# A short first chunk, and the recurrent stage's elementwise work moved from GpSimd to VectorE and ScalarE

## The chip, the core and the metric

The kernel runs on one core of a Trainium2 chip. The metric is device time in microseconds (us), from one launch. Engines are named as the profile names them: PE is TensorE, PEld its weight loads, DVE is VectorE, ACT is ScalarE, POOL is GpSimd, and SP is SyncE, which here issues all DMAs.

## What is computed

One layer of a hybrid decoder for a prompt of 4096 positions and for 8 single-token samples. All is fp32. The reference, cut to what matters here:

```python
xn = rms_norm(x, norm_pre)                       # x: 4096 x 1024 (prompt), 8 x 1024 (samples)
proj = xn @ w_in                                 # 1024 x 2304
x_rnn, g_rnn, q, k, v, g_att = split(proj)       # 512, 512, 512, 128, 128, 512
xc = causal_conv(x_rnn, width 4)                 # depthwise, along positions
r, i = sigmoid(blockdiag(xc) + b_a), sigmoid(blockdiag(xc) + b_x)
a = exp(-8 r softplus(-lam))
h_t = a_t h_{t-1} + sqrt(1 - a_t^2) (i_t xc_t)   # scan over positions
rnn_out = h * silu(g_rnn)
att_out = window_attention(q, k, v, window 128, sinks, bias) * silu(g_att)
y = x + rms_norm(concat(rnn_out, att_out) @ w_out, norm_post)
```

The samples go through the same layer, each from its own convolution state, recurrent state and key/value window. The new states and windows are outputs too.

## The kernel before, in words

Positions lie along the columns, and a *chunk* is the unit of all stages. `chunk_list` (L38) cuts 4096 positions into ten chunks of 384 (`STEP`) and a last one of 256; the eight samples ride as columns 256 to 263 of that last chunk. A chunk is thus 384 or 264 columns wide. Every fp32 product is made of three matmuls of rounded high and low parts (`mm3`, L121 to L124).

**Stage A, the recurrent heads**, one chunk after another. `load_A` (L146) loads x in tiles of 128 rows (the samples are a tile of 8 rows), takes the mean square (ACT, L161; in the first chunk's second tile DVE, L157), its root on POOL (L141), and scales the tile by it: on DVE in the first chunk (L164), on POOL in all others (L166). `prep_A` transposes the tile on PE (L176) and splits it into high (ACT, L179) and low parts (DVE, L180), which are also stored to DRAM (`xT_d`, L182) for stage B. `proj_A` makes two projections for each of four groups c of 128 channels (L122 to L124; 8 x 24 matmuls a chunk), evacuates them (ACT, L298, L302, L316), makes three convolution taps on DVE (L304; for the samples L309), and splits the result xc into xk (L312, L313). `rnn_A` makes the two gate products from xk (24 matmuls a chunk), the tanh and exp on ACT (L333 to L338), and on DVE and POOL the pieces of the recurrence: L339, L341 and L342 on DVE, `aa` (L340) on POOL. `scan_A` takes the square root on ACT (L348), then for each c multiplies `ix` by it (POOL, L350), scans (DVE, L352), and multiplies by the gate (POOL, L361); SP stores the result to `mix_d` (L362). The tiles named thi in the trace are `ix`. The projections of the very first group are L210 to L213, in another order.

The eight weight blocks of stage A (512 KB each) are loaded, rounded (ACT, L111, or DVE, L109) and their low parts taken (DVE, or POOL, L112) during the first chunk.

**Stage B, attention**, again chunk by chunk: ten projections of 24 matmuls (V, K, four Q, four G), and a unit for each pair of key head and 128-query block: scores (L601, L602), masked minimum and softmax on DVE and ACT (L619 to L632), transposes (L635), triangular cuts on POOL (L654, L656), the product with the values (L661), and the gate (POOL, L676). kt (L484, L486, L524) holds split keys, sq (L564 to L567) split queries. The ten weight blocks of stage B are loaded from the end of stage A on; their low parts are taken on POOL (L112). The samples' keys, values, queries and gates are taken out of the projections' last 8 columns (L531, L546, L571, L584).

**Stage C, the output product**: eight blocks of w_out are loaded, `mix_d` is read back and split (`prep_B`, L189, L193, L195), and each tile of 128 positions is multiplied (L817 to L819), normalized, added to x and stored. `attend_sample` runs the samples' attention in five pieces between chunks and stores it to `mix_d`; the samples' tile is put between the two prompt tiles of the chunk that carries them, and that chunk's last tile ends the kernel.

What sets the order: `A_ORDER` (L33), `B_FIRST` (L35) and `B_ORDER` (L36) are the orders in which a chunk's pieces are emitted, P a projection, L the x loads and X a quarter of the preparation of the next chunk, R the gates and S the scans; U units, M their gates.

```python
A_ORDER = "P1 L P0 P2 R1 X0 R0 P3 X1 R2 X2 R3 S X3".split()
```

The build then orders each engine's queue by a timeline of its own (`schedule_with_timeline_sim=True`), so that pieces that follow each other here are interleaved in the trace. Each queue runs in its order. PSUM has four projection buffers in stage A and two in stage B.

Of the kernel before, what the change touches and what calls it, by code (L numbers as in the profile page):

```python
# [12 lines left out]
AF = mybir.ActivationFunctionType  # L13
ALU = mybir.AluOpType
# [10 lines left out]
NSAMP = 8  # L25
SEQ = 4096
STEP = 384
# [8 lines left out]


def chunk_list():  # L38
    out = [(t, min(STEP, SEQ - t), 0) for t in range(0, SEQ, STEP)]
    out[-1] = out[-1][:2] + (NSAMP,)  # L40
    return out


@with_exitstack
def hymba_kernel(ctx: ExitStack, tc: tile.TileContext, ins, outs):
    nc = tc.nc
# [9 lines left out]
    w_out_v = w_out[0].rearrange("(e p) d -> p e d", p=P)  # L56

    chunks = chunk_list()
    NCH = len(chunks)

    act = nc.scalar.activation
# [16 lines left out]
    def ps_s(n):  # L78
        if phase[0] == "A":
            return ps[1].tile([P, 1024], F32, tag="s", name=n, bufs=1)  # L80
        return ps[0].tile([P, 1024], F32, tag="s", name=n, bufs=2)
# [15 lines left out]
    mix_d = [dram.tile([P, KD, n + s], F32, name=f"mix_d{i}") for i, (_, n, s) in enumerate(chunks)]  # L97
# [23 lines left out]
    def mm3(out, wh, wl, xh, xl, first, last):  # L121
        nc.tensor.matmul(out, wh, xh, start=first, stop=False)  # L122
        nc.tensor.matmul(out, wh, xl, start=False, stop=False)  # L123
        nc.tensor.matmul(out, wl, xh, start=False, stop=last)  # L124
# [10 lines left out]
    def rstd(pool, ss, rows, n):  # L135
        nc.vector.tensor_scalar(ss[:rows], ss[:rows], EPS, None, op0=ALU.add)
        return root(pool, ss, rows, n)

    def root(pool, ss, rows, n):
        rs = pool.tile([P, 1], F32, tag="rs", name=f"rs_{n}", bufs=4)  # L140
        nc.gpsimd.tensor_tensor(rs[:rows], ss[:rows], mhalf[:rows], op=ALU.pow)  # L141
        return rs


    def load_A(pool, ci):
        t0, npt, ns = chunks[ci]  # L146
        tiles = [(x_p[t0 + i * P:t0 + (i + 1) * P, :], P, i * P) for i in range(npt // P)]
        if ns:
            tiles.append((x_s, ns, npt))
        xn = []  # L150
        for j, (src, rows, off) in enumerate(tiles):
            xs = pool.tile([P, D], F32, tag="xs", name=f"xs_{ci}_{j}", bufs=4)
            nc.sync.dma_start(xs[:rows], src)
            ss = pool.tile([P, 1], F32, tag="ss", name=f"ss_{ci}_{j}", bufs=4)
            if ci == 0 and j == 1:
                sq = pal.tile([P, D], F32, tag="uu", name=f"sq_{ci}_{j}", bufs=1)
                nc.vector.tensor_tensor_reduce(sq[:rows], xs[:rows], xs[:rows], op0=ALU.mult, op1=ALU.add,  # L157
                                               scale=1.0 / D, scalar=0.0, accum_out=ss[:rows])
            else:
                sq = pool.tile([P, D], mybir.dt.bfloat16, tag="sq", name=f"sq_{ci}_{j}", bufs=1)  # L160
                act(sq[:rows], xs[:rows], AF.Square, scale=1.0 / 32.0, accum_out=ss[:rows])  # L161
            rs = rstd(pool, ss, rows, f"{ci}_{j}")
            if ci == 0:
                nc.vector.tensor_scalar(xs[:rows], xs[:rows], rs[:rows], None, op0=ALU.mult)  # L164
            else:
                nc.gpsimd.tensor_scalar(xs[:rows], xs[:rows], rs[:rows], 1.0, op0=ALU.mult, op1=ALU.mult)  # L166
            xn.append((xs, rows, off))
        return xn

# [28 lines left out]
    cms = [tc.tile_pool(name=n, bufs=1) for n in ("pa_late", "pa", "prep")]  # L198
    pal, pa, prep = [c.__enter__() for c in cms]
    xn = load_A(prep, 0)  # L200

    def project2(w1, w2, xs, W, n, wait=False):
# [73 lines left out]
    at = spp.pop()  # L276
# [44 lines left out]
    def rnn_A(pool, ci, c, uu, xc, xk, sg):  # L321
        t0, npt, ns = chunks[ci]
        W = npt + ns
        pg = ps_s(f"gt_{ci}_{c}")
        for g in range(2):
            o = pg[:, g * 512:g * 512 + W]
            mm3(o, gwh[:, 2 * c + g, :], gwl[:, 2 * c + g, :], xk[:, 0, :W], xk[:, 1, :W], True, True)

        def wt(tag, bufs=2, pool=pool):
            return pool.tile([P, STEP], F32, tag=tag, name=f"{tag}_{ci}_{c}", bufs=bufs)[:, :W]  # L330

        thr, thi = wt("thr", 3, pal), wt("thi", 4, pal)
        act(thr, pg[:, 0:W], AF.Tanh, scale=0.5, bias=hba[:, c:c + 1])  # L333
        act(thi, pg[:, 512:512 + W], AF.Tanh, scale=0.5, bias=hbx[:, c:c + 1])

        tt, aa = wt("tt", 2, pal), wt("aa", 4, pal)
        act(tt, thr, AF.Tanh, scale=sp2[:, c:c + 1], bias=sp2[:, c:c + 1])
        act(thr, thr, AF.Exp, scale=sp4n[:, c:c + 1], bias=sp4n[:, c:c + 1])  # L338
        nc.vector.scalar_tensor_tensor(thr, thr, 1.0, tt, op0=ALU.add, op1=ALU.mult)  # L339
        nc.gpsimd.tensor_scalar(aa, thr, -1.0, 1.0, op0=ALU.mult, op1=ALU.add)  # L340
        nc.vector.scalar_tensor_tensor(uu[:, c, :W], thr, 2.0, thr, op0=ALU.subtract, op1=ALU.mult)  # L341
        nc.vector.scalar_tensor_tensor(thi, thi, 1.0, xc[:, :W], op0=ALU.add, op1=ALU.mult)  # L342
        return aa, thi, sg

    def scan_A(pool, ci, uu, parts):
        t0, npt, ns = chunks[ci]
        W = npt + ns
        act(uu[:, :, :W], uu[:, :, :W], AF.Sqrt, scale=-0.25)  # L348
        for c, (aa, ix, sg) in enumerate(parts):
            nc.gpsimd.tensor_mul(ix, ix, uu[:, c, :W])  # L350
            hh = pal.tile([P, STEP], F32, tag="hh", name=f"hh_{ci}_{c}", bufs=4)
            nc.vector.tensor_tensor_scan(hh[:, :npt], aa[:, :npt], ix[:, :npt], hprev[c] if ci else 0.0,  # L352
                                         op0=ALU.mult, op1=ALU.add)
            hprev[c] = const.tile([P, 1], F32, tag=f"hl{c}", name=f"hl_{ci}_{c}", bufs=2)
            nc.gpsimd.tensor_copy(hprev[c], hh[:, npt - 1:npt])
            if ns:
                o = hh[:, npt:W]
                nc.vector.tensor_mul(o, aa[:, npt:W], h0T[:, c, :])
                nc.vector.tensor_add(o, o, ix[:, npt:W])
                nc.gpsimd.tensor_copy(hs[:, c, :], o)  # L360
            nc.gpsimd.tensor_mul(hh[:, :W], hh[:, :W], sg[:, :W])  # L361
            nc.sync.dma_start(mix_d[ci][:, c, :], hh[:, :W])  # L362


# [76 lines left out]
    for ci in range(NCH):  # L441
        for item in A_ORDER:
            f, s = item[0], st[ci]
            c = int(item[1:] or 0)
# [237 lines left out]
    def attend_sample(pool):  # L682
# [51 lines left out]
        at = pool.tile([P, 4, NSAMP], F32, name="at_s")  # L734
# [2 lines left out]
                act(at[par * HD:(par + 1) * HD, 2 * kv:2 * kv + 2, :],  # L737
                    pov[kv * HD:(kv + 1) * HD, par, 2 * kv:2 * kv + 2, :], AF.Copy)
        nc.vector.scalar_tensor_tensor(at, at, 0.5, sgS, op0=ALU.mult, op1=ALU.mult)
        n = chunks[-1][1]  # L740
        nc.sync.dma_start(mix_d[-1][:, 4:8, n:n + NSAMP], at)

    for c in reversed(pcms):
        c.__exit__(None, None, None)
# [26 lines left out]

    wC = [load_w_out(e) for e in range(8)]
    sample = attend_sample(pb)
    turn = 0
    for ci in range(NCH):
        t0, npt, ns = chunks[ci]
        mh, ml = prep_B(ci, mix_d[ci], True, range(4))
        tiles = [(x_p[t0 + i * P:t0 + (i + 1) * P, :], y_p[t0 + i * P:t0 + (i + 1) * P, :], P, i * P)
                 for i in range(npt // P)]
# [9 lines left out]
            tiles.insert(1, (x_s, y_s, NSAMP, 0))  # L789
        for j, (xsrc, ydst, rows, off) in enumerate(tiles):  # L790
            n = f"{ci}_{j}"
            final = ci == NCH - 1 and j == len(tiles) - 1
            xr = stage.tile([P, D], F32, tag="ws", name=f"xr2_{n}")[:rows]
            nc.sync.dma_start(xr, xsrc)
            if final:
# [47 lines left out]
            rs = root(const, ss[:, 0:1], rows, f"c{n}")  # L843
# [4 lines left out]
                    nc.sync.dma_start(ydst[:, c[0]:c[1]], o)  # L848
            if not final:
                nc.sync.dma_start(ydst, xr)  # L850
        if ci:
            next(sample, None)
    for c in reversed(pcms):
        c.__exit__(None, None, None)
# [22 lines left out]
def build(nc, arrays):  # L877
    args = []
    for name in _INS + ['onehot']:
        a = arrays[f"in_{name}_dram"]  # L880
        args.append(nc.dram_tensor(f"in_{name}_dram", a.shape, mybir.dt.from_np(a.dtype), kind="ExternalInput").ap())
    res = []
    for i, (shape, dtype) in enumerate(_OUTS):
        res.append(nc.dram_tensor(f"out_{i}_dram", shape, F32, kind="ExternalOutput").ap())
    with tile.TileContext(nc, schedule_with_timeline_sim=True) as tc:
        hymba_kernel(tc, args, res)
# [13 lines left out]
```

## Time and profile before

| | us |
|---|---|
| runs, median of 3 (lowest to highest) | 1454.05 (1452.31 to 1455.19) |
| the profiled execution's own time | 1454.09 |
| its span, first to last instruction | 1452.4 |
| PE busy in the span | 1408.3 |
| DVE, ACT, POOL busy | 908.6, 798.7, 604.6 |

A share of busy time says how much an engine works, not whether it sets the end. For that one looks for stretches in which the engine that works most stands still, and for what ended its wait. The granted clock beside a stretch is the mean of TensorE's clock in it, as a share of 2.4 GHz. By PE's lines, stage A runs to some 475 us, stage B to some 1100 us, and stage C to the end.

### The profile page before, as it was taken

What the parts mean: (1) busy time and instruction counts of PE and PEld (TensorE: products, weight loads), DVE (VectorE), ACT (ScalarE), POOL (GpSimd) and SP (SyncE); (2) the same over time, 40 slices, a digit from 0 to 9 for tenths busy, and PEclk for the clock granted to TensorE, in tenths of its full rate; (3) what the DMA queues carried; (4) which work ended last, traced back from release to release, by engine and by line L of the source; (5) the groups of instructions that cost most, each with busy time, mean ns of one, the idle gap of its engine ahead of it and who ended that gap; (6) DMA issues with size and microseconds to landing.
All of it is one profiled execution on the core that took longest, in us unless ns stands there. A gap on an engine that the chain in (4) does not pass through costs nothing.

```text
span 1452.4 us, 24152 instructions
## 1 busy us (share of the span) xinstructions
PE 1408.3 (97%) x8127; PEld 1326.6 (91%) x8127; DVE 908.6 (63%) x2108; ACT 798.7 (55%) x2055; POOL 604.6 (42%) x1026
## 2 busy tenths in 40 slices
PE   6999999999988889999999999999999999999998
PEld 5999999999988889999999999999988888888886
DVE  5788777777878756576575575575665445334433
ACT  4656656666645566766776776776864222222211
POOL 3366665555656633544543543543762000000000
PEclk9999999999999999999999999999999999999999
DMA  8343354443324520221212212212336534433431
GB/s 271 127 157 133 131 168 148 142 152 120 122 73 145 184 79 31 99 85 67 99 46 76 98 42 79 98 38 70 107 111 196 172 131 145 141 135 131 146 130 60
DMA packets 115029, 170.24 MB, mean 117 GB/s; under 512 B 12214, under 2 KB 98822, under 8 KB 114906
## 3 DMA queue, kind: packets, MB, share of 16 engines
q1 hardware_dynamic: 114906, 168.71, 34.6%
q8 instruction: 64, 1.05, 0.3%
q14 instruction: 59, 0.48, 0.1%
HBM read 100.19 MB, written 68.50 MB: 116 GB/s over the span
## 4 chain that ended last, share of the span: by engine, by line
PE 83%; DVE 5%; ACT 4%; DMA 3%; issue 3%; POOL 1%; SPq 1%; POOLq 0%; DVEq 0%; ACTq 0%
PE out L817 8%; PE out L818 8%; PE out L819 8%; PE pr L122 6%; PE pr L124 6%; PE pr L123 6%; PE pga L122 4%; PE pga L123 4%; PE pga L124 4%; PE pq L122 4%; PE pq L123 4%; PE pq L124 4%; PE po L661 3%; PE S L601 2%; PE S L602 2%
## 5 line engine op out<-in xcount | busy, mean ns | idle before, releaser
L123 PE MATMUL pr<-xl,wh_in 128*128 128x384 f32 (+1 forms) x688 | 231.6, 337 | 0.0
L124 PE MATMUL pr<-xh,wl_in 128*128 128x384 f32 (+1 forms) x688 | 228.9, 334 | 0.0
L122 PE MATMUL pr<-xh,wh_in 128*128 128x384 f32 (+1 forms) x688 | 218.7, 336 | 0.9 <-ACT xc L302 0.6
L817 PE MATMUL out<-wh_out,xh_mix_d 128*128 128x512 f32 (+1 forms) x520 | 201.0, 387 | 0.0
L818 PE MATMUL out<-wl_out,xh_mix_d 128*128 128x512 f32 (+1 forms) x520 | 200.9, 386 | 0.0
L819 PE MATMUL out<-wh_out,xl_mix_d 128*128 128x512 f32 (+1 forms) x520 | 200.9, 386 | 0.0
L141 POOL TENSOR_TENSOR rs_c<-ssc,mhalf 128x1 f32<-128x1 f32 (+1 forms) x33 | 20.4, 620 | 322.5 <-DVE ssc L840 294.6
L836 ACT ACTIVATE sqc<-out 128x512 bf16<-128x512 f32 (+2 forms) x67 | 39.2, 585 | 194.6 <-PE out L819 184.4
L627 ACT ACTIVATE tt<-tt,nm 128x129 f32<-128x129 f32 x256 | 100.0, 393 | 77.2 <-DVE nm L624 76.7
L839 DVE TENSOR_TENSOR out<-out,gpost 128x512 f32<-128x512 f32 (+1 forms) x65 | 45.4, 698 | 144.2 <-ACT sqc L836 143.6
L123 PEld LDWEIGHTS pr<-xl,wh_in 128*128 128x128 f32 x688 | 131.3, 191 | 0.7 <-issue 0.7
L122 PEld LDWEIGHTS pr<-xh,wh_in 128*128 128x128 f32 x688 | 129.8, 191 | 2.1 <-ACT xc L302 1.8
L124 PEld LDWEIGHTS pr<-xh,wl_in 128*128 128x128 f32 x688 | 131.2, 191 | 0.3 <-issue 0.2
L122 PE MATMUL pq<-xh_B,wh_in 128*128 128x384 f32 (+1 forms) x352 | 119.5, 339 | 7.7 <-DVE kt L486 4.8
L123 PE MATMUL pga<-xl_B,wh_in 128*128 128x384 f32 (+1 forms) x352 | 119.1, 338 | 0.0
L123 PE MATMUL pq<-xl_B,wh_in 128*128 128x384 f32 (+1 forms) x352 | 118.9, 338 | 0.0
L124 PE MATMUL pq<-xh_B,wl_in 128*128 128x384 f32 (+1 forms) x352 | 118.6, 337 | 0.0
L304 DVE SCALAR_TENSOR_TENSOR xc<-xr,cT,xc 128x384 f32<-128x384 f32 (+1 forms) x132 | 113.0, 862 | 8.6 <-ACT xc L302 5.9
L122 PE MATMUL pga<-xh_B,wh_in 128*128 128x384 f32 (+1 forms) x352 | 118.3, 336 | 0.0
L124 PE MATMUL pga<-xh_B,wl_in 128*128 128x384 f32 (+1 forms) x352 | 117.5, 334 | 0.0
L817 PEld LDWEIGHTS out<-wh_out,xh_mix_d 128*128 128x128 f32 x520 | 97.6, 188 | 19.8 <-issue 0.2
L819 PEld LDWEIGHTS out<-wh_out,xl_mix_d 128*128 128x128 f32 x520 | 97.7, 188 | 19.6
(258 smaller groups left out, 3711.2 us busy)
## 6 DMA issues: line engine op xcount, KB each, us to landing
xs<-in_x_prompt_dram SPq DMA_DIRECT2D x32, 512.0 KB
xr<-in_x_prompt_dram SPq DMA_DIRECT2D x32, 512.0 KB
out_dram<-xr SPq DMA_DIRECT2D x31, 512.0 KB
xT_d<-xh SPq DMA_DIRECT2D x80, 192.0 KB
xT_d<-xl SPq DMA_DIRECT2D x80, 192.0 KB
xf_mix_d<-mix_d SPq DMA_DIRECT2D x80, 192.0 KB
xh_B<-xT_d SPq DMA_DIRECT2D x80, 192.0 KB
xl_B<-xT_d SPq DMA_DIRECT2D x80, 192.0 KB
```

Source lines behind the costliest of these rows:

```text
L122: nc.tensor.matmul(out, wh, xh, start=first, stop=False)
L123: nc.tensor.matmul(out, wh, xl, start=False, stop=False)
L124: nc.tensor.matmul(out, wl, xh, start=False, stop=last)
L304: nc.vector.scalar_tensor_tensor(xc[:, :npt], xr[:, t:t + npt], cw[:, t, c:c + 1], xc[:, :npt], op0=ALU.mult, op1=ALU.add)
L601: nc.tensor.matmul(o, qa, kt[:, kv, 0, kr], start=True, stop=False)
L627: act(tt[:, g, 0:P + 1], tt[:, g, 0:P + 1], AF.Exp, scale=-1.0, bias=nm[:, g:g + 1], accum_out=sm[:, g:g + 1])
L661: nc.tensor.matmul(pog[:, :, r], v.rearrange("p l d -> p (l d)"), w[:, :, r], start=i == 0, stop=i == 2)
L817: nc.tensor.matmul(p, a, wh, start=st, stop=False)
L818: nc.tensor.matmul(p, a, wl, start=False, stop=False)
L819: nc.tensor.matmul(p, b, wh, start=False, stop=sp)
L836: act(sq[:rows, :c[1] - c[0]], p[:rows], AF.Square, scale=1.0 / 32.0, accum_out=ss[:rows, i:i + 1])
L839: nc.vector.tensor_mul(po[i][:rows], p[:rows], gpost[:rows, c[0]:c[1]])
```

## The change

The short chunk, with the samples, becomes the first one; stage C takes it last. In stage A four kinds of operation change their engine: the scaling of x from POOL to ACT, and `aa`, `ix` times the root, and the scan's product with the gate from POOL to DVE. POOL keeps the root of the mean square, small copies and the weights' low parts. The chunk order of stages A and B is 0 to 10 as before, now with widths 264, 384, ..., 384.

```diff
 def chunk_list():
-    out = [(t, min(STEP, SEQ - t), 0) for t in range(0, SEQ, STEP)]
-    out[-1] = out[-1][:2] + (NSAMP,)
-    return out
+    first = SEQ % STEP
+    return [(0, first, NSAMP)] + [(t, STEP, 0) for t in range(first, SEQ, STEP)]
...
             if ci == 0:
                 nc.vector.tensor_scalar(xs[:rows], xs[:rows], rs[:rows], None, op0=ALU.mult)
             else:
-                nc.gpsimd.tensor_scalar(xs[:rows], xs[:rows], rs[:rows], 1.0, op0=ALU.mult, op1=ALU.mult)
+                act(xs[:rows], xs[:rows], AF.Copy, scale=rs[:rows])
...
-        nc.gpsimd.tensor_scalar(aa, thr, -1.0, 1.0, op0=ALU.mult, op1=ALU.add)
+        nc.vector.tensor_scalar(aa, thr, -1.0, 1.0, op0=ALU.mult, op1=ALU.add)
...
-            nc.gpsimd.tensor_mul(ix, ix, uu[:, c, :W])
+            nc.vector.tensor_mul(ix, ix, uu[:, c, :W])
...
-            nc.gpsimd.tensor_mul(hh[:, :W], hh[:, :W], sg[:, :W])
+            nc.vector.tensor_mul(hh[:, :W], hh[:, :W], sg[:, :W])
...
-        n = chunks[-1][1]
-        nc.sync.dma_start(mix_d[-1][:, 4:8, n:n + NSAMP], at)
+        n = chunks[0][1]
+        nc.sync.dma_start(mix_d[0][:, 4:8, n:n + NSAMP], at)
...
-    for ci in range(NCH):
+    order = [*range(1, NCH), 0]
+    for ci in order:
...
-            final = ci == NCH - 1 and j == len(tiles) - 1
+            final = ci == order[-1] and j == len(tiles) - 1
...
-        if ci:
+        if ci != order[0]:
             next(sample, None)
```

## Rows read from the trace of the kernel before

**Rows 1.** The page's part 1: each engine's busy time, share, instructions.

```profile
PE 1408.3 (97%) x8127; PEld 1326.6 (91%) x8127; DVE 908.6 (63%) x2108; ACT 798.7 (55%) x2055; POOL 604.6 (42%) x1026
```

**Rows 2.** Busy time by stretch: PE, PEld, DVE, ACT, POOL, granted clock, DMA, GB/s.

```profile
99.00:386.00 287.00, 285.85 (x1684) 280.44 (x1683) 228.91 (x361) 182.49 (x315) 176.49 (x213) 1.00 0.41 141
...
415.00:428.00 13.00, 9.21 (x34) 7.93 (x33) 11.06 (x21) 4.54 (x9) 4.57 (x8) 0.74 0.22 76
...
459.00:472.00 13.00, 8.51 (x43) 7.99 (x44) 13.00 (x19) 3.30 (x6) 11.12 (x14) 0.74 0.49 149
...
492.00:503.00 11.00, 6.24 (x27) 6.07 (x26) 10.86 (x18) 3.34 (x7) 8.95 (x14) 0.69 0.28 83
...
514.00:527.00 13.00, 8.43 (x40) 8.12 (x39) 9.12 (x30) 10.85 (x36) 4.80 (x3) 0.74 0.01 1
...
1038.00:1066.00 28.00, 23.56 (x174) 22.45 (x173) 16.08 (x50) 21.42 (x61) 20.09 (x26) 0.94 0.35 118
```

**Rows 3.** Waits of PE: us in total, times, the longest.

```profile
PE gt L122 <- DVE xk L312: 6.4, 2, 3.9
PE pq L122 <- DVE kt L486: 4.8, 1, 4.8
...
PE S L601 <- DVE sq L566: 3.5, 1, 3.5
PE gt L123 <- DVE xk L313: 2.4, 3, 1.3
```

**Rows 4.** Timeline of DVE from 403 us: start, duration, operation, count.

```profile
408.40 0.59 DVE L304 SCALAR_TENSOR_TENSOR xc<-xr,cT,xc 128x384 f32<-128x384 f32 x1
...
410.29 7.52 DVE L304 SCALAR_TENSOR_TENSOR xc<-xr,cT,xc 128x384 f32<-128x384 f32 x4
417.73 0.34 DVE L312 CAST xk<-xc 128x384 fp32r<-128x384 f32 x1
```

**Rows 5.** Timeline of POOL in the same stretch.

```profile
410.65 1.13 POOL L166 TENSOR_SCALAR xs<-xs,rs 128x1024 f32<-128x1024 f32 x1
411.75 1.96 POOL L361 TENSOR_TENSOR hh<-hh,sg 128x384 f32<-128x384 f32 x2
```

**Rows 6.** Groups of DVE, 36 to 475 us: busy us, mean ns, idle before.

```profile
L304 DVE SCALAR_TENSOR_TENSOR xc<-xr,cT,xc 128x384 f32<-128x384 f32 x120 | 102.8, 863 | 8.6 <-ACT xc L302 5.9 <-POOL aa L340 2.6
L352 DVE TENSOR_TENSOR_SCAN hh<-aa,hl,thi 128x384 f32<-128x384 f32 x36 | 55.5, 1563 | 2.7 <-POOL thi L350 2.7
...
L313 DVE TENSOR_TENSOR xk<-xc,xk 128x384 fp32r<-128x384 f32 x40 | 22.5, 563 | 0.3
```

**Rows 7.** Timeline of PE: three matmuls in a row, the first of 264 columns.

```profile
473.99 0.28 PE L124 MATMUL pr<-xh,wl_in 128*128 128x264 f32 x1
474.11 0.34 PE L124 MATMUL pv<-xh_B,wl_in 128*128 128x384 f32 x1
474.28 0.33 PE L122 MATMUL pv<-xh_B,wh_in 128*128 128x384 f32 x1
```

**Rows 8.** Groups of POOL, 36 to 475 us.

```profile
L350 POOL TENSOR_TENSOR thi<-thi,uu 128x384 f32<-128x384 f32 x40 | 51.8, 1326 | 23.9 <-ACT uu L348 23.9
L361 POOL TENSOR_TENSOR hh<-hh,sg 128x384 f32<-128x384 f32 x40 | 49.4, 1246 | 0.0
L166 POOL TENSOR_SCALAR xs<-xs,rs 128x1024 f32<-128x1024 f32 x28 | 39.9, 1426 | 0.2
...
L340 POOL TENSOR_SCALAR aa<-thr 128x384 f32<-128x384 f32 x40 | 27.0, 675 | 106.8 <-DVE thr L339 106.8
```

**Rows 9.** A group of ACT, 36 to 475 us.

```profile
L161 ACT ACTIVATE sq<-xs 128x1024 bf16<-128x1024 f32 x28 | 29.5, 1053 | 9.3 <-DMA xs<-in_x_prompt_dram 9.1
```

**Rows 10.** Timeline of DVE, at the change from stage A to B.

```profile
499.29 2.54 DVE L524 CAST kt<-kt 128x512 fp32r<-128x512 f32 x1
```

**Rows 11.** Timeline of POOL at the same time.

```profile
498.77 2.77 POOL L112 TENSOR_TENSOR wl_in<-ws_in,wh_in 128x1024 fp32r<-128x1024 f32 x1
```

**Rows 12.** Timeline of PE at the start.

```profile
14.24 0.69 PE L176 MATMUL pt<-ident,xs 128*128 128x128 f32 x2 [2.88 <-DVE xs L164]
```

## The prediction

> **What bounds the kernel now.** I read the engine line first, then the busy time by stretch, then TensorE's waits, and last the timelines of VectorE (DVE) and GpSimd (POOL) in the stretches where TensorE (PE) stands. PE is busy 1408.3 us of 1452.4 [rows 1]. In the middle of stage A (99 to 386 us) it issues 1684 matmuls, which are seven full chunks of 192 + 24 + 24, and lacks 1.15 us of 287 at full granted clock [rows 2]: there no other engine's work is worth anything while its cover lasts. A chunk takes 41.0 us, and of these DVE is busy 228.91 / 7 = 32.7, ScalarE (ACT) 26.1, POOL 25.2 [rows 2].
>
> What can be won is in five stretches where PE idles and the granted clock then falls from the 2.4 GHz level to the 1.2 GHz one for some us. From rows 2, idle plus (1 - granted clock) x length, the clock being the stretch's mean:
> - 415 to 428: 3.79 + 0.26 x 13 = 7.2 us
> - 459 to 472: 4.49 + 3.4 = 7.9 us
> - 492 to 503: 4.76 + 0.31 x 11 = 8.2 us
> - 514 to 527: 4.57 + 3.4 = 8.0 us
> - 1038 to 1066: 4.44 + 0.06 x 28 = 6.1 us
>
> The first two are PE's gate products of stage A waiting for DVE's split xk, 6.4 us in two waits, with 2.4 more for its low part; the third is a query projection waiting for DVE's kt, 4.8 us; the fourth is scores waiting for DVE's sq, 3.5 us [rows 3]. So DVE is late each time, though on average it has time to spare.
>
> Why it is late shows in the timelines. A convolution tap (L304) takes 0.59 us at 408.40, but the four that follow at 410.29 take 7.52 us [rows 4]. In just that time POOL runs the xs scaling and the hh products back to back [rows 5]. Over the stage the tap's mean is 863 ns [rows 6]. So POOL's elementwise work is not free: it holds DVE's.
>
> **The change part by part.**
>
> *Columns.* The chunks are the same lengths in another order. A matmul of 264 columns takes 0.12 us of the queue and one of 384 takes 0.17 us [rows 7], 0.45 ns a column both ways. PE's work is conserved: 0 us.
>
> *The twelve elementwise operations of a chunk (L340, L350, L361, four each) go from POOL to DVE.* POOL loses 4 x (1.33 + 1.25 + 0.68) = 13.0 us a chunk [rows 8]. No row has them on DVE. The nearest is L313, a two-input fp32 operation of DVE on the same shape: 0.563 us. The lower bound is 0.34, a one-input cast of that shape [rows 4] (aa has one input too); the upper is the scan's mean under POOL, 1.563 [rows 6]. I take 0.56, since POOL will hardly run beside them: 12 x 0.56 = 6.8 us. On the other side, 12 taps come down from 0.863 to 0.59: 3.3 us [rows 4, 6]; what the scan and the cast win I leave uncounted. DVE comes to 32.7 + 6.8 - 3.3 = 36.2 of 41.0 us. PE still covers it, so 0 us in the steady chunks, and perhaps 0.5 of their 1.15 us of idle. If PE's cover were gone, the net 3.5 us would cost a chunk just that.
>
> *The xs scaling (L166) goes from POOL to ACT.* Three a chunk; the nearest ACT row of that shape is the square, 1.053 us [rows 9]; POOL's is 1.426 [rows 8]. ACT: 26.1 + 3.2 = 29.3 of 41.0 us. Hidden by PE. Behind it in ACT's queue wait PSUM evacuations, by 1.05 us at a time, which four PSUM buffers of 24 matmuls x 0.17 = 4.2 us each cover. Bounds: 0 to 1 us a chunk. I take 0.
>
> *SP.* The mix_d stores (L362) wait for the same product, now a DVE one; behind them in SP's queue stand the next chunk's x loads and xT_d stores. The product ends earlier if DVE is not held. 0 us.
>
> *415 to 428.* This stall is POOL's hold on DVE and nothing else [rows 4, 5]. It goes: -7.2 us, bounds 0 and -7.2.
>
> *459 to 472.* The same wait, in the short last chunk, with scans and sample operations on DVE. The last chunk is now a full one without samples, and POOL no longer multiplies. -7.9 us, bounds 0 and -7.9.
>
> *492 to 503 and 514 to 527, from stage A to stage B.* DVE's tail of stage A stands in front of kt. It loses POOL's hold, but now carries 384 columns and eight products (8 x 0.56 = 4.5 us). PE has less to bridge it with: stage B's first chunk is 264 wide, so a projection is 24 x 0.12 = 2.9 us, not 4.2; four are 5 us less cover. The sample's small evacuations move here too. I take +2 for the pair, bounds -16.2 (both go) and +11.4 (5 at each place, and 1.4 of deeper clock loss).
>
> The row that speaks against this: POOL keeps its weight subtractions here, and a cast of DVE took 2.54 us beside one of 2.77 us [rows 10, 11]. The Trainium skill, GPSIMD Engine Reference, section 8 (Key points), says that GpSimd shares its SBUF interfaces with VectorE and contends with its instructions in a two-port mode or with two SBUF inputs; the moved operations are of these kinds. By that rule, with two of them held as the cast was, this term would be about +4.4 and the time 1440.4; the trace has the hold for the old operations, and no row shows it for the moved ones.
>
> *1038 to 1066, from stage B to stage C.* The last chunk of stage B becomes full: its ten projections last 41.6 us instead of 28.8 beside the same eight loads of w_out, and the sample's evacuations leave. Half of it goes: -3 us, bounds 0 and -6.1.
>
> *Start.* Two full x tiles and eight sample rows instead of three tiles. The transposes wait 2.88 us for the third tile's scaling [rows 12]: most of that goes, -2.5. But the eight weight loads of stage A now have 192 matmuls x 0.12 = 23 us of projections to hide behind, not 33. If they come no sooner, PE waits up to 10 us more. DMA has less x and xT_d to move then, so I take a third, +3. Net +0.5, bounds -2.9 and +10.
>
> *End.* The last chunk of stage C has the same form as before (two tiles and the sample's): 0.
>
> Sum: -0.5 - 7.2 - 7.9 + 2 - 3 + 0.5 = -16.1 us. The profiled execution took 1454.09 us (span 1452.4), which is the median of the runs, 1454.05, within 0.04. So 1438.0 us.
>
> **The rivals.**
>
> *A. Forecast*: POOL's hold goes and the two stalls of stage A with it; the change of stages stays about as it is. 1431 to 1446. Chance 0.54.
>
> *B. The stall moves to the change of stages or to the start.* The narrow first chunk covers less of both. For it: DVE's tail is the releaser there [rows 3]. Against: DVE's tail shortens. With +11.4 in place of +2, the sum is -6.7: 1447.4; with a few us more at the start, 1450. Chance 0.18.
>
> *C. The tail shortens so much that one of the two stalls between A and B goes too.* -8.2 in place of +2: 1427.8. For it: VectorE's tail is held by POOL now [rows 10, 11]. Chance 0.15.
>
> *D. Slower: DVE becomes the bound in stage A.* It has 41.0 - 32.7 = 8.3 us a chunk left; that is used up when the twelve cost over 0.69 us each with no relief elsewhere. At the tap's held price, 0.863, they cost 10.4: 2.1 us over, in ten full chunks +21, and the two stalls stay. With +2, -3 and +0.5 from above, +20.5: 1474.6. Against: what holds DVE is the very work that is taken from POOL. Chance 0.06.
>
> *E. No change.* The burst of products and scans on DVE at the end of a chunk delays xk as POOL's hold did, and the two stalls stay: -0.5 + 2 - 3 + 0.5 = -1, 1453, give or take the 4 us by which these four small terms may be off. Against: 8 x 0.56 us is less than the 7.52 us of rows 4. Chance 0.07.
>
> **How the numbers follow.** 0.2% (2.9 us) is about what a measurement of this kernel can tell from no change. A (0.54), C (0.15) and 0.16 of B are faster: 0.85. Most of E and 0.02 of B, 0.08, are within; D and the rest of E, 0.07, slower. The range leaves out D, E, the top of B and the low tail of C, about 2 in 10: 1426 to 1450. It reaches to C and B, and so takes in either bound of the largest unknown, the change from A to B, not the bounds of all terms at once. The likeliest case's own range is 1431 to 1446.
>
> **What would show it.** Right: L304's mean near 0.6 us; POOL's share down by about 17 us a chunk; no stretch of half clock in stage A after its start; PE's waits for xk gone; DVE near 36 us a chunk. Wrong: xk still the releaser of the gate products; a chunk longer than 41.0 us in the middle of stage A (D); PE's idle between A and B over 20 us (B); or idle in the first chunk over 10 us more than now, released by weights or by ACT.

## The result, and the profile after

The change makes the kernel slower: 1467.35 us (median of 5 runs, 1462.34 to 1470.59) against 1454.05 before, a ratio of 1.0084 with a 95% interval of 1.0057 to 1.0110. The forecast was 1438.0, faster. The profiled execution took 1470.59 us, with a span of 1468.9 (before: 1452.4). It is the slowest of the five; the readings below take from it where the time lies, not its last microsecond.

The engine line of the page, after, answers to [rows 1]:

```profile
PE 1414.4 (96%) x8127; PEld 1333.5 (91%) x8127; DVE 897.8 (61%) x2240; ACT 827.9 (56%) x2085; POOL 449.4 (31%) x864
```

POOL lost 155 us and ACT gained 29, as meant. DVE took twelve operations a chunk more and is busy for 11 us less in all, so POOL's work had held DVE's. The groups of DVE after, 100 to 430 us (busy us, mean ns, idle before), answer to [rows 6]:

```profile
L304 DVE SCALAR_TENSOR_TENSOR xc<-xr,cT,xc 128x384 f32<-128x384 f32 x87 | 51.1, 610 | 3.2 <-ACT xc L302 3.2
...
L352 DVE TENSOR_TENSOR_SCAN hh<-aa,hl,thi 128x384 f32<-128x384 f32 x32 | 30.5, 1002 | 0.0
L361 DVE TENSOR_TENSOR hh<-hh,sg 128x384 f32<-128x384 f32 x32 | 16.9, 548 | 0.1
...
L350 DVE TENSOR_TENSOR thi<-thi,uu 128x384 f32<-128x384 f32 x32 | 15.7, 553 | 19.4 <-ACT uu L348 19.4
...
L340 DVE TENSOR_SCALAR aa<-thr 128x384 f32<-128x384 f32 x29 | 10.4, 358 | 0.7
L312 DVE CAST xk<-xc 128x384 fp32r<-128x384 f32 x28 | 9.6, 353 | 13.7 <-PE gt L124 13.7
```

In the same 330 us of the kernel before, the tap's mean was 883 ns, the scan's 1485 and the cast's (L312) 692. They fell to 610, 1002 and 353, and the moved operations cost 553, 548 and 358. Yet PE stands more. Busy time by stretch, of the kernel before and then of the kernel after (start to end, length, then busy us of PE, PEld, DVE, ACT, POOL, each with its instructions, granted clock, DMA share, GB/s):

```profile
60.00:400.00 340.00, 338.28 (x1998) 332.35 (x1997) 268.65 (x428) 215.73 (x373) 205.64 (x247) 1.00 0.42 143
400.00:560.00 160.00, 141.97 (x837) 137.15 (x836) 112.79 (x231) 90.67 (x203) 84.04 (x118) 0.91 0.35 113
```

```profile
60.00:400.00 340.00, 326.10 (x1870) 319.74 (x1869) 240.28 (x500) 226.78 (x374) 79.74 (x127) 0.97 0.39 133
...
400.00:440.00 40.00, 37.62 (x213) 36.98 (x212) 27.49 (x56) 22.81 (x38) 10.24 (x13) 0.96 0.37 126
440.00:560.00 120.00, 104.53 (x633) 101.53 (x632) 91.51 (x180) 71.88 (x159) 42.65 (x47) 0.90 0.41 128
...
1020.00:1100.00 80.00, 79.03 (x501) 77.92 (x500) 54.70 (x177) 64.91 (x199) 57.16 (x93) 1.00 0.35 114
```

Idle plus (1 - clock) x length, in the middle of stage A: 1.7 us before, 13.9 + 0.03 x 340 = 24 after. The chunk went from 41.0 to 44.8 us (the square roots, L348, start at 149.0 us and, five chunks later, at 373.1). From 400 to 560 us: 18.0 + 14.4 = 32 before, 4.0 + 27.5 = 32 after. From B to C 1.0 us are left of 6.1 [rows 2]. Stage A's steady chunks alone carry more than the whole loss of 16.5 us of span. What PE waited for there, after (us in total, times, longest):

```profile
PE pt L176 <- ACT xs L166: 8.8, 5, 2.3
PE pr L122 <- ACT xc L302: 5.1, 6, 3.1
```

The waits for xk that the forecast was about are all but gone (0.7 us over the span). In their place stand two waits for ACT: the transposes of the next x wait for its scaling, which before stood on POOL, and a projection waits for `xc`, the evacuation (L302) of an earlier one, 5.1 us in place of 0.6. Where both stand at one change of chunks, the evacuation is done after the scaling and ends the wait. ACT's timeline after, at one change of chunks:

```profile
188.70 0.72 ACT L338 ACTIVATE thr<-thr,sp4n 128x384 f32<-128x384 f32 x1
191.98 1.06 ACT L161 ACTIVATE sq<-xs 128x1024 bf16<-128x1024 f32 x1 [2.55 <-DMA xs<-in_x_prompt_dram]
...
193.14 1.28 ACT L348 ACT_TABLE_LOAD   x1
194.44 1.49 ACT L348 ACTIVATE uu<-uu 128x1536 f32<-128x1536 f32 x1
195.83 1.03 ACT L161 ACTIVATE sq<-xs 128x1024 bf16<-128x1024 f32 x1
...
196.87 1.13 ACT L166 ACTIVATE xs<-xs,rs 128x1024 f32<-128x1024 f32 x1
197.91 0.47 ACT L298 ACTIVATE xr<-pr 128x384 f32<-128x384 f32 x1
198.28 0.66 ACT L302 ACTIVATE xc<-pr,cT 128x384 f32<-128x384 f32 x1
```

PE, in the same stretch:

```profile
195.60 0.34 PE L124 MATMUL pr<-xh,wl_in 128*128 128x384 f32 x1
198.99 0.69 PE L122 MATMUL pr<-xh,wh_in 128*128 128x384 f32 x1 [3.05 <-ACT xc L302]
```

PE had finished the projections of the new chunk's first two groups, two for each, which fill all four PSUM buffers, and could not begin the third group's until ACT had emptied the first's. ACT came to that only behind a square that waited for its x, a table load, the square root, another square and a scaling. The table load began at 193.14 us, though the square root's last input (DVE, L341) had been ready since 190.87: the square in front of it held it. Then the clock falls from the 2.4 GHz level to the 1.2 GHz one; two stretches of the kernel after:

```profile
195.00:199.00 4.00, 0.95 (x7) 0.63 (x5) 3.04 (x7) 3.98 (x7) 0.56 (x3) 1.00 0.47 167
199.00:202.00 3.00, 3.00 (x9) 3.00 (x10) 3.00 (x4) 2.99 (x6) 3.00 (x4) 0.50 0.96 270
```

Before, ACT's queue at the same place reads: exp, table load and square root first, then two squares, then the evacuation. The scaling is on POOL there, and no square stands in front of the square root.

```profile
237.34 1.28 ACT L348 ACT_TABLE_LOAD   x1
238.63 1.49 ACT L348 ACTIVATE uu<-uu 128x1536 f32<-128x1536 f32 x1
240.09 1.06 ACT L161 ACTIVATE sq<-xs 128x1024 bf16<-128x1024 f32 x1
...
242.12 1.06 ACT L161 ACTIVATE sq<-xs 128x1024 bf16<-128x1024 f32 x1 [0.89 <-DMA xs<-in_x_prompt_dram]
...
243.55 0.66 ACT L302 ACTIVATE xc<-pr,cT 128x384 f32<-128x384 f32 x1
```

It ended at 244.21. The third group's projection began at 244.80 without a wait:

```profile
244.80 0.42 PE L122 MATMUL pr<-xh,wh_in 128*128 128x384 f32 x1
```

That is a margin of 0.6 us, which no view of busy shares shows.

### The profile page after: what moved, and what is told of

It reads as the page before. It is cut to its first block, busy times and chain, and to the rows that moved or that the text cites. A ratio compares the mean times of both kernels' runs of the same rounds, so it can differ in the third digit from the quotient of the medians.

```text
span 1468.9 us, 24089 instructions
## 1 busy us (share of the span) xinstructions
PE 1414.4 (96%) x8127; PEld 1333.5 (91%) x8127; DVE 897.8 (61%) x2240; ACT 827.9 (56%) x2085; POOL 449.4 (31%) x864
## 3 DMA queue, kind: packets, MB, share of 16 engines
q8 instruction: 64, 1.05, 0.3%
## 4 chain that ended last, share of the span: by engine, by line
PE 87%; ACT 4%; DMA 3%; DVE 3%; issue 2%; SPq 1%; POOL 0%; POOLq 0%; DVEq 0%; ACTq 0%
PE out L819 8%; PE out L820 8%; PE out L821 8%; PE pr L122 7%; PE pr L123 6%; PE pr L124 6%; PE pga L122 4%; PE pga L123 4%; PE pga L124 4%; PE pq L122 4%; PE pq L123 4%; PE pq L124 4%; PE po L661 3%; DMA xs<-in_x_prompt_dram 2%; PE S L601 2%; PE S L602 2%
## 5 line engine op out<-in xcount | busy, mean ns | idle before, releaser
L123 PE MATMUL pr<-xl,wh_in 128*128 128x384 f32 (+1 forms) x688 | 234.8, 342 | 0.0
L122 PE MATMUL pr<-xh,wh_in 128*128 128x384 f32 (+1 forms) x688 | 224.2, 344 | 9.4 <-ACT xc L302 7.1
L141 POOL TENSOR_TENSOR rs_c<-ssc,mhalf 128x1 f32<-128x1 f32 (+1 forms) x33 | 20.4, 619 | 319.1 <-DVE ssc L842 290.7
L820 PEld LDWEIGHTS out<-wl_out,xh_mix_d 128*128 128x128 f32 x520 | 97.7, 188 | 19.1
```

Source lines behind the costliest of these rows:

```text
L820: nc.tensor.matmul(p, a, wl, start=False, stop=False)
```

## The experiments

The parts are C (the short chunk first), D (the twelve operations to DVE) and X (the scaling to ACT). The kernel before has none and the full change is CDX. A run's name lists its parts. The theories of the expectations: T1, X delays x in every chunk; T2, the moved operations on DVE delay PE; T3, the narrow first chunk costs at the start and from A to B. The others came with the later runs and are told there.

**One or two parts at a time.**

```diff
# c_only: CDX without D and X    x_only: before with X    d_only: before with D
# cd: CDX with the scaling back on POOL
-                act(xs[:rows], xs[:rows], AF.Copy, scale=rs[:rows])
+                nc.gpsimd.tensor_scalar(xs[:rows], xs[:rows], rs[:rows], 1.0, op0=ALU.mult, op1=ALU.mult)
```

> The changed kernel with the xs scaling back on GpSimd; chunk order and the twelve moved VectorE operations stay. Theory 1 (the scaling in ScalarE's queue makes the next chunk's x late, and TensorE waits for it in each chunk of stage A): the about 26 us that stage A lost over its middle chunks come back, 1441 us (1436 to 1447), and TensorE has no wait for xs in the middle of stage A. Theory 2 (the moved products on VectorE delay what TensorE needs): within 5 us of the changed kernel, 1462 to 1472. Theory 3 (the narrow first chunk costs at the start and at the change to stage B): also within 5 us of the changed kernel.

> The kernel before with the xs scaling on ScalarE alone. Theory 1: some 4 us a chunk in the middle of stage A, 1475 us (1466 to 1484), with TensorE waiting for xs scaled at line 166. Theories 2 and 3: 1454 us within 4, or a few us faster, since GpSimd holds VectorE less.

> The kernel before with the twelve operations of a chunk on VectorE alone. Theory 1: the hold of GpSimd on VectorE goes and with it the stalls at 415 and 459 us, 1442 us (1436 to 1450). Theory 2: slower than before by 10 us or more, 1464 to 1475. Theory 3: 1442, as theory 1.

> The kernel before with the short chunk first alone. Theory 3: slower than before by 10 us or more, from the start and from the change to stage B. Theories 1 and 2: about the same, 1449 us (1444 to 1457): 6 us won at the change to stage C, up to 4 lost at the start.

Measured, beside before at 1453.51 us: cd 1453.9 (ratio 0.9996, 0.9984 to 1.0008), x_only 1450.52 (0.9978, 0.9969 to 0.9988), d_only 1453.46 (1.0001, 0.9987 to 1.0015), c_only 1445.83 (0.9949, 0.9935 to 0.9964). T3 falls, since C alone gains 8 us. T2 falls, since D alone costs nothing. T1 falls as it was put: X alone gains 3 us. But X added to CD costs 13. No part is guilty by itself, and no theory gave a range that holds the time of cd.

**The two pairs that were missing, and two edits of the full change.** T4 blames PE's early reads of the new x, T5 ACT's load.

```diff
# cx: CDX without D        dx: CDX without C
# cdx_hold1: the roots of the tiles after the first need the first gate product sg too
+            mh = pool.tile([P, 1], F32, tag="mh", name=f"mh_{ci}", bufs=2)
+            nc.gpsimd.tensor_scalar(mh, late[:, 0:1], 0.0, -0.5, op0=ALU.mult, op1=ALU.add)
...
-        nc.gpsimd.tensor_tensor(rs[:rows], ss[:rows], mhalf[:rows], op=ALU.pow)
+        nc.gpsimd.tensor_tensor(rs[:rows], ss[:rows], (mh or mhalf)[:rows], op=ALU.pow)
...
-                    s["n"] = load_A(prep, ci + 1)
+                    s["n"] = load_A(prep, ci + 1, s["p", 1][2])
# cdx_bufs6
-            xs = pool.tile([P, D], F32, tag="xs", name=f"xs_{ci}_{j}", bufs=4)
+            xs = pool.tile([P, D], F32, tag="xs", name=f"xs_{ci}_{j}", bufs=6)
```

> Parts C (short chunk first) and X (xs scaling on ACT) without D (the twelve operations stay on POOL). Alone, C took 8 us off, X 3, D 0, but C with D took 0 and all three added 13. Two new theories. T4: D makes the built order of PE read the next chunk's second x tile early, 7.4 us of matmuls after the last read of the old x, where before, X alone and C alone have 18.0; with X that tile's scaling stands in ACT's queue behind the square root and is not done by then, so PE waits in every chunk. T5: it is ACT's load: the scaling and the wait for rs hold the PSUM evacuations, whatever PE's order is, once the short chunk comes first. Here PE's order has 18.0 us. T4: stage A stays without waits, the two gains add, 1443 us (1440 to 1447). T5: stage A loses a few us a chunk, 1458 or more.

> Parts D and X, the chunks in the old order. PE's built order reads the second x tile 7.4 us after the last read of the old one, as in the full change. T4: the same waits as in the full change, stage A loses some 20 us, 1466 us (1460 to 1472), though D alone and X alone took 0 and 3 us off. T5: without C no loss, 1451 (1447 to 1456).

> The full change, and the roots rs of the second and third x tile are made to need the chunk's first gate product sg too (one small POOL operation a chunk more), so that x is ready later and PE's built order reads the second tile at 16.2 us instead of 7.4. No work leaves ACT or DVE. T4: x later makes the kernel faster: PE's waits for xs go, stage A loses at most 9 us, 1453 us (1448 to 1458). T5: nothing leaves ACT's queue and x comes later, so 1467 or more.

> The full change with six xs buffers for four, so that all three tiles of the next chunk can be loaded, squared and scaled before the old ones are read for the last time. PE's order still reads the second and third tile early (7.2 and 7.3 us). T4: the reads are early but x is ready, so PE's waits for xs go: 1453 us (1447 to 1458). T5: ACT does the same work in the same queue, 1464 to 1470.

Measured, before at 1454.31: cx 1444.08 (0.9935, 0.9920 to 0.9950), dx 1462.93 (1.0066, 1.0051 to 1.0081), cdx_hold1 1452.65 (0.9984, 0.9971 to 0.9998; its runs spread from 1446.48 to 1455.56), cdx_bufs6 1475.5 (1.0150, 1.0135 to 1.0165). So D and X together make the loss, whatever the order of the chunks, and making x *later* takes some 15 us off the full change. D, which costs nothing alone, costs wherever another part is there: 8 us with C (cd against c_only), 12 with X (dx against x_only), 23 with both (the full change against cx). T5 had cx, dx and hold1 wrong, and put cdx_bufs6 at least 5 us too low. T4 had cdx_bufs6 wrong by 22 us. Its waits between 60 and 400 us show how; they have a single row over 0.1 us:

```profile
PE pr L122 <- ACT xc L302: 23.1, 9, 4.0
```

The wait for the scaling went, as T4 said, and the wait for the evacuation rose from 5.1 us to 23.1. ACT's timeline in that run:

```profile
251.11 1.49 ACT L348 ACTIVATE uu<-uu 128x1536 f32<-128x1536 f32 x1
252.51 1.04 ACT L161 ACTIVATE sq<-xs 128x1024 bf16<-128x1024 f32 x1
...
253.54 1.13 ACT L166 ACTIVATE xs<-xs,rs 128x1024 f32<-128x1024 f32 x1
254.59 0.47 ACT L298 ACTIVATE xr<-pr 128x384 f32<-128x384 f32 x1
254.96 0.66 ACT L302 ACTIVATE xc<-pr,cT 128x384 f32<-128x384 f32 x1
```

This led to T7: it is the place in ACT's queue. Between the square root and the evacuation a scaling stands, in the third to the tenth chunk, in every one of dx, in all but the third of CDX and all but the tenth of cdx_bufs6, and in none of any other kernel here. T7 was put to four new kernels.

**Four kernels chosen by the order of ACT's queue.** Each moves nearly as much work as the full change or has one of its suspects.

```diff
# cdx_no361: CDX with L361 back on POOL
-            nc.vector.tensor_mul(hh[:, :W], hh[:, :W], sg[:, :W])
+            nc.gpsimd.tensor_mul(hh[:, :W], hh[:, :W], sg[:, :W])
# cdx_no340: CDX with L340 back on POOL      cx_bufs6: cx with six xs buffers
# cx_361: cx with L361 alone on DVE
```

> The full change with the four hh products (L361) back on POOL; L340 and L350 stay on DVE, the scaling on ACT, the short chunk first. T4 had PE's waits for xs right in the run with six buffers (they went), but the time rose to 1475: PE waited 23 us for ACT's PSUM evacuation xc instead. T7: what counts is the order in ACT's queue at the change of chunks. In the full change and with six buffers, one scaling (and squares) stands between the square root uu and the evacuation of the new chunk's first projection, which PE needs for its third one; in every run without the loss that evacuation stands in front of all scalings. Here it does (uu, two squares, evacuation, then the scalings). T7: stage A loses at most 9 us between 60 and 400, 1446 us (1441 to 1453). T9, the rival: DVE's added load and ACT's added load do it together, whatever the order: two thirds of the added DVE work stay, so 1457 or more.

> The full change with the four cheapest of the twelve operations (L340, 0.36 us each on DVE) back on POOL. In ACT's queue the scalings again stand behind the first evacuation, though PE still reads x early (second tile 12.6 or 15.4 us after the last read of the old x). T7: 1449 us (1442 to 1455). T9: 1.4 us a chunk less for DVE changes little, 1463 or more.

> Short chunk first and the scaling on ACT, the twelve operations on POOL, and six xs buffers for four. ACT's queue at the change of chunks: uu, two squares, evacuation, as without the buffers; PE reads all three tiles at 8.5 us. T7: no loss in stage A, 1444 us (1440 to 1449). If it is the six buffers themselves that cost (early loads and early reads), 1460 or more, as in the full change with them.

> Short chunk first, scaling on ACT, and of the twelve operations only the four hh products (L361) on DVE, the part whose return the first run of this call tries. Evacuation in front of all scalings in ACT's queue. T7: 1443 us (1438 to 1450), so L361 is not the guilty part by itself. T9: about a third to a half of the loss of 19 us against the pair without it, 1450 or more.

Measured, before at 1453.58: cdx_no361 1439.52 (0.9913, 0.9893 to 0.9933), cdx_no340 1443.38 (0.9929, 0.9914 to 0.9944), cx_bufs6 1440.83 (0.9911, 0.9897 to 0.9926), cx_361 1439.8 (0.9905, 0.9891 to 0.9920). All four are without the loss; T7 was right in kind four times, though 3 to 6.5 us too high, so that cdx_no361 lies just under its range; T9 was wrong in the three that it priced. Returning the four cheapest operations (L340) takes 24 us off the full change. The load of neither engine explains that: between 60 and 400 us both DVE (250 us for 240) and ACT (246 for 227) are busier there than in the full change. PE between 60 and 400 us in cdx_hold1, cdx_bufs6 and cdx_no361, in this order:

```profile
60.00:400.00 340.00, 336.09 (x1989) 331.22 (x1988) 251.06 (x523) 240.22 (x394) 81.50 (x136) 1.00 0.41 143
```

```profile
60.00:400.00 340.00, 316.92 (x1795) 311.51 (x1794) 233.40 (x486) 221.74 (x363) 73.22 (x124) 0.95 0.39 132
```

```profile
60.00:400.00 340.00, 338.75 (x2011) 335.32 (x2010) 263.79 (x504) 246.81 (x405) 114.46 (x169) 1.00 0.42 144
```

The same column for all kernels, PE's idle time in these 340 us: before 1.7, c_only 1.9, x_only 0.9, cx 1.2, d_only 6.1, cd 6.9, hold1 3.9, no361 1.3, no340 1.0, cx_bufs6 0.9, cx_361 0.1; and dx 15.3, CDX 13.9, cdx_bufs6 23.1. ACT in cdx_no361, which is busier there (246.81 us) than in the full change (226.78):

```profile
227.53 1.28 ACT L348 ACT_TABLE_LOAD   x1
228.82 1.49 ACT L348 ACTIVATE uu<-uu 128x1536 f32<-128x1536 f32 x1
231.25 1.06 ACT L161 ACTIVATE sq<-xs 128x1024 bf16<-128x1024 f32 x1 [0.94 <-DMA xs<-in_x_prompt_dram]
...
234.10 0.67 ACT L302 ACTIVATE xc<-pr,cT 128x384 f32<-128x384 f32 x1
...
236.47 1.14 ACT L166 ACTIVATE xs<-xs,rs 128x1024 f32<-128x1024 f32 x1
```

The evacuation ends at 234.77, and PE's third group begins at 235.04 without a wait. Here the margin is 0.3 us.

T7 is not the whole account. d_only, cd and cdx_hold1 have no scaling at that place, yet wait for the same evacuation between 60 and 400 us, 5.7, 6.5 and 3.9 us in all. ACT and PE at one such change in d_only:

```profile
322.88 1.06 ACT L161 ACTIVATE sq<-xs 128x1024 bf16<-128x1024 f32 x1 [1.75 <-DMA xs<-in_x_prompt_dram]
...
328.14 0.66 ACT L302 ACTIVATE xc<-pr,cT 128x384 f32<-128x384 f32 x1
```

```profile
328.85 0.44 PE L122 MATMUL pr<-xh,wh_in 128*128 128x384 f32 x1 [1.87 <-ACT xc L302]
```

The square that waits for its x stands in front of the square root, as in the full change. The 14 kernels have 140 changes of chunks in stage A. PE's waits for the scaled x and for the evacuation, taken together at each:

| at the change of chunks | changes | with a wait | mean wait, us |
|---|---|---|---|
| no square in front of the square root, no scaling between | 103 | 4 | 0.0 |
| a square in front, no scaling between square root and evacuation | 14 | 14 | 1.5 |
| a square in front and a scaling between | 23 | 22 | 2.4 |

The one without a wait in the last row is the second chunk of cx_bufs6. So the larger part of the wait goes with the square that holds the square root back, and some 0.9 us more with the scaling (1.15 us long). Between 60 and 400 us the granted clock is 0.97, 0.97 and 0.95 in CDX, dx and cdx_bufs6, which have both at most changes, and 1.00, 0.99 and 1.00 in d_only, cd and cdx_hold1, which have the square alone at four or five. The traces of d_only and cdx_hold1 are of fast executions of theirs (1449.94 and 1446.48 us), so in others they may wait more.

What stays open: no kernel here has the scaling at that place without a square in front, so the two were not separated by a run of their own. One of them forced into a kernel without the loss, all else as it was, was not tried: the build orders the queues anew with every edit. Nor is it shown why the build puts the square in front of the square root with D, and not when L340 or L361 goes back to POOL.

## Why the prediction was wrong

**The step that failed is the scaling's**: "Behind it in ACT's queue wait PSUM evacuations, by 1.05 us at a time, which four PSUM buffers of 24 matmuls x 0.17 = 4.2 us each cover. Bounds: 0 to 1 us a chunk. I take 0." The price was right (1.15 us in the trace for 1.05) and so was the load (ACT is busy 66% of a chunk, 29.5 us for 29.3). The cover (4.1 us by these figures) was not there. At the change of chunks the projections of the first two groups are interleaved and end together, so all four buffers fill at about the same time, and the margin was 0.6 us. What took it is two things: the square moved ahead of the square root, which waits there for its x, and the scaling's 1.13 us behind it. The prediction has the second and puts it at 0; the first, which comes with D (36 of the 37 changes that have it are in kernels with D), it does not have: it looked at the load of DVE and ACT, not at the order of ACT's queue. PE's idle is 13.9 us for 1.7, and lost clock makes 10 of the 24 us. Together 22 us more than before in this stretch, where the text had -0.5 for D and X. One of its signs of being wrong came true: a chunk longer than 41.0 us.

**The hold on DVE** was right as a mechanism and too small in size. The sum had DVE at 36.2 us a chunk. It was 165.66 us in the 240 us from 140 to 380, so 30.9 in a chunk of 44.8, in part because the scan and the cast, left uncounted, came down too. So rival D, DVE as the bound, had the right sign, with 1474.6, by luck: its reason did not exist.

**The end of stage A and the change from A to B**, three terms, were to bring -13.1 us; the stretch from 400 to 560 us gave nothing (32 us before and after). The stall at 415 to 428 went, but the chunk changes of stage A now cost there too (4.0 us from 400 to 440). The one at 459 to 472 came back in another form: POOL's weight subtractions (L112) held the scans and two products of the last chunk but one, and PE waited 2.3 us for DVE's sg (L318) and 0.7 for xk at 477 to 480 us. And stage B's first chunk, narrow and with the samples, waits for the evacuations of its projections; PE's waits after, from 400 to 560 us:

```profile
PE pga L122 <- DVE sgb L582: 4.9, 1, 4.9
PE pga L122 <- ACT qz L571: 4.4, 1, 4.4
...
PE pq L122 <- ACT qz L571: 1.8, 1, 1.8
```

Together 11.1 us, in place of 4.8 and 3.5 for kt and sq [rows 3]. The releaser behind them is DVE. ACT stood idle before the 4.4 us wait's qz until DVE's sq, which stood behind the scans and products of stage A's last chunk; and sgb came after softmax work of DVE beside a weight subtraction. ACT, DVE and POOL:

```profile
521.81 0.37 ACT L571 ACTIVATE qz<-pq 64x8 f32<-64x8 f32 x2 [3.16 <-DVE sq L567]
```

```profile
464.15 8.08 DVE L352 TENSOR_TENSOR_SCAN hh<-aa,hl,thi 128x384 f32<-128x384 f32 x4
...
473.13 2.88 DVE L361 TENSOR_TENSOR hh<-hh,sg 128x384 f32<-128x384 f32 x2
...
532.10 2.79 DVE L632 TENSOR_TENSOR tt<-tt,ri 128x512 f32<-128x512 f32 x1
```

```profile
472.75 2.39 POOL L112 TENSOR_TENSOR wl_in<-ws_in,wh_in 128x1024 fp32r<-128x1024 f32 x1
...
531.97 2.37 POOL L112 TENSOR_TENSOR wl_in<-ws_in,wh_in 128x1024 fp32r<-128x1024 f32 x1 [11.04 <-ACT wh_in L111]
```

A wait of this kind (pga for sgb or qz, 1.6 to 9.3 us in all) is in each of the ten kernels with the short chunk first and in none of the other four: it goes with C. This is rival B's place, though not its sum: B had 11.4 us for the pair and nothing lost in the middle of stage A.

The Trainium skill, GPSIMD Engine Reference, section 8 (Key points), lets GpSimd contend with VectorE at a shared SBUF interface when the latter has two SBUF inputs or a two-port mode. These rows agree, and give a size: 2.88 us for two products that take 0.55 us each without a subtraction beside them, 8.08 us for four scans of 1.00. The hold fell only on what ran beside POOL's work: of the eight L361 from 440 to 560 us the other six took 0.55 us, and L350 kept its 553 ns.

**B to C** was right in sign and within its bounds (-5.1 for -3). **The start** cost 2.1 us (13.1 us of PE's idle in the first 60 before, 15.2 after) for +0.5. **The end** was right, within 0.6.

Without the failed step the time comes near the forecast of 1438.0: cdx_no361 has all three parts but four operations and takes 1439.5 us, cx_361 1439.8, both faster than before by 14 us. With cx_bufs6 (1440.8) they are the best of the kernels run. That cdx_no361 comes so near is partly luck. By the same reckoning its stretch from 400 to 560 us takes 23 us (16.7 idle, clock 0.96), so it gave -9 and not -13.1, with a wait of 6.3 us for xk still in it.

## What to carry to other kernels

- A share of busy time shows whether an engine has room for an operation, not whether there is room at the place in its queue where the operation will stand. Find the place where the engine that sets the end waits least for this one (here 0.6 us), and price the operation there, with what may stand in front of it waiting for a transfer.
- Where the build orders the queues itself, an edit on one engine reorders the others. Two edits that are harmless alone (0 and -3 us here) can cost 9 together, so test pairs, and compare the order of the queues beside the times.
- A resource that frees an input earlier (six buffers) can cost as much as it saves if the order then uses it earlier: some 8 us more in one kernel here, 3 less in another.

## What the hardware showed unexpectedly

- POOL's elementwise work holds more of DVE than the taps. The scan fell by a third (1485 to 1002 ns) and the one-input cast by half (692 to 353), with no edit to either. From 100 to 430 us the scan's mean is 1.00 us in d_only, cd and dx and 1.48 to 1.49 in x_only, c_only and cx, so it goes with D.
- A short wait of PE can be followed by half clock, and need not be: after 3.05 us of idle in the full change the clock was 0.50 (the 1.2 GHz level) for 3 us, with PE busy all through; after 2.34 us in cdx_hold1 (to 402.8 us) it stayed at 1.00.
- The hold goes both ways. In the kernel after, POOL's root of one column (L141) took 0.55 us where DVE stood, 0.85 beside two taps and 1.31 beside three scans; a copy of three columns (L295) took 0.18 us beside one DVE operation and 2.33 beside six in a row (at 177.38). On average, from 100 to 430 us, the copy took 961 ns after and 743 before, the root 911 and 801. The copy's rise is not D's as such: in d_only, with the same operations on DVE, its mean is 431.
